# First value product from channel-scaled x, row factor at eviction, and one written order for the keys' end

## The chip, the cores and the metric

The kernel runs on one core of a Trainium2 chip. The metric is the device time of one execution in microseconds (us). Engines are named as in the profile: PE is TensorE's matmul stream and PEld its weight loads, DVE is VectorE, ACT is ScalarE, POOL is GpSimd, SP is SyncE, which only issues transfers. A queue carries its engine's name with a q behind it.

## The reference

One layer of an encoder block, 1024 tokens by 1024 channels, in fp32. The part that matters here is its head:

```python
mod = c_act @ ada_w[l] + ada_b[l]              # c_act = silu(c), one row
sh1, sc1, g1, sh2, sc2, g2 = split(mod, 6)
h = rmsnorm(x, ln1_g[l]) * (1.0 + sc1) + sh1
p = h @ w_in[l]
q, k, v, cb, cc, cx, ga, gb = split(p, ...)
q = rmsnorm(q per head, q_norm_g[l]);  k = rmsnorm(k per head, k_norm_g[l])
```

Behind it come a stick-breaking attention, a short gated convolution, gates, an output projection and a SwiGLU feed-forward part. `rmsnorm` divides each token's row by its root mean square, so `h = r * x * a + sh1` with one factor `r` for a token and one factor `a = ln1_g * (1 + sc1)` for a channel.

## The kernel before

Every product of two fp32 matrices is made from two rounded halves of each side (`hi` and `lo`), as three matmuls: hi by hi, hi by lo, lo by hi. ACT makes a hi, DVE a lo.

The head has these parts. (1) Eight tiles of x, tokens on partitions, are loaded (L173), squared on ACT with a running sum (L242), and give the row factor by a power on POOL (L111). Eight matmuls per half turn the row factors into a row broadcast over all partitions (`bcast`, L249). (2) Per channel tile k, two reductions of 1024 columns on DVE give shift and scale (`mod_sum`, L225, from the transfers `ada`), `norm_x` (L260) multiplies the channel-major x (`xts`) by both factors, `make_hi` and `make_lo` (L265, L269) make the halves of h in the four large tiles `hh` and `hl`. (3) The first value product (512 of 1024 value columns) runs k by k into eight PSUM banks at once: 8 token tiles by 3 matmuls for each k (`real`, L308), the last k token by token, each followed by its eviction and store (`finish_v`, L394). (4) Two key products (two times 512 columns) run token tile by token tile, 24 matmuls each, `finish_k` (L373) behind each: squares on ACT, sums per head on DVE, a power on POOL, `qn` on DVE, four transposes on PE, halves of the key, two stores. (5) `factors` (L341) makes, from x in place, sums and differences of quadrants of h for the gates' seven-product (Strassen-like) scheme and stores four sets as halves (`ts`, three buffers, to `d_t`); h's first half of channels for the later tokens is saved (`d_h`). It is a generator; `more` (L418) takes two or three of its steps behind each key tile. (6) The sets come back as `ft` (two of them before, one after the gates begin) and over the saved half of h. The first gates' two early products (`first_two`, L504, 48 matmuls) need only h.

Instructions are put in order by a planner with its own costs and due times, but for the part from `i0` to L411, which `in_order` (L142) holds in written order on every engine. The planner therefore orders parts (4) to (6). ACT, DVE and POOL take their instructions strictly in the order they are given, and so do the queues.

## Time and profile before

| what | us |
|---|---|
| median of 3 runs (1828.74 to 1829.21) | 1829.14 |
| the profiled execution | 1830.01 |
| its span from first to last instruction | 1828.2 |
| PE busy in the span | 1797.8 |
| DVE busy | 1344.4 |
| ACT busy | 780.1 |

The profiled execution is one run, here 0.9 us above the median. Its own time holds the span and 1.8 us around it. Busy time of PE counts pipelined matmuls whose ends are modelled. The chain of waits follows the work that ended last back to its releasers; it tells which engine a stretch hangs on.

### The profile page before, as it was taken

Reading aid. Unit: us, or ns where it says so; the run is one execution under the profiler, and the core shown is the slowest. Engines: PE = TensorE matmul, PEld = TensorE weight load, DVE = VectorE, ACT = ScalarE, POOL = GpSimd, SP = SyncE. Lnnn points to the kernel's source line nnn. Section 1 sums busy time; section 2 is a strip of 40 time slices with the busy share of each in tenths; the row PEclk is TensorE's granted clock in tenths of the full one; section 3 lists DMA queues with packets and bytes.
Section 4 is the critical chain, followed back from the end, with each engine's and each line's share of the span. In section 5 each row is a group of like instructions: output and inputs, shape, how many; then the busy total and the mean of one; then the engine's idle time right before and its main releaser. Section 6 shows DMA issues by size and latency. Waiting matters only on the chain.

```text
span 1828.2 us, 24681 instructions
## 1 busy us (share of the span) xinstructions
PE 1797.8 (98%) x8765; PEld 1497.7 (82%) x8765; DVE 1344.4 (74%) x1873; ACT 780.1 (43%) x1463; POOL 498.2 (27%) x373
## 2 busy tenths in 40 slices
PE   7999999999999999999999999999999999999999
PEld 5788777888889988888888888878888888878887
DVE  5874686777954888888887584589987788653774
ACT  4342454333344656665655212353443344422320
POOL 0043433833322122211210001335545445200000
PEclk9999999999999999999999999999999999999999
DMA  9688544222738576668544674505443344299776
GB/s 388 212 301 273 192 151 141 93 75 81 259 115 247 145 199 192 187 196 227 160 141 150 217 245 163 174 23 185 184 173 139 138 173 161 93 353 319 279 241 213
DMA packets 148145, 347.23 MB, mean 190 GB/s; under 512 B 15003, under 2 KB 52141, under 8 KB 145846
## 3 DMA queue, kind: packets, MB, share of 16 engines
q1 hardware_dynamic: 112368, 244.79, 41.5%
q10 hardware_dynamic: 30678, 84.61, 12.3%
q0 software_dynamic: 4976, 16.26, 2.4%
q8 instruction: 70, 1.15, 0.3%
q14 instruction: 53, 0.43, 0.1%
HBM read 238.11 MB, written 107.48 MB: 189 GB/s over the span
## 4 chain that ended last, share of the span: by engine, by line
PE 88%; DVE 6%; DMA 2%; issue 2%; ACT 2%; POOL 1%; SPq 0%; DVEq 0%; POOLq 0%; ACTq 0%
PE e L119 7%; PE e L120 7%; PE e L121 7%; PE pj L121 7%; PE pj L119 7%; PE pj L120 7%; PE pj L284 5%; PE e L1506 4%; PE e L1508 4%; PE e L1507 4%; PE tr L817 3%; PE pj L887 3%; PE pj L888 3%; PE pj L889 3%; PE obank L833 2%
## 5 line engine op out<-in xcount | busy, mean ns | idle before, releaser
L802 DVE TENSOR_TENSOR_SCAN pt<-pt,mk 128x128 f32<-128x128 f32 (+7 forms) x128 | 179.6, 1411 | 48.5 <-ACT pt L798 48.1
L124 DVE TENSOR_TENSOR wlo<-raw,whi 128x512 fp32r<-128x512 f32 x148 | 125.5, 857 | 47.4 <-ACT whi L439 35.0
L798 ACT ACTIVATE pt<-z,rq 128x512 f32<-128x512 f32 (+3 forms) x192 | 107.9, 579 | 88.0 <-PE z L797 60.7
L119 PE MATMUL e<-big,whi 128*128 128x512 f32 x352 | 138.1, 392 | 1.1 <-DVE c L124 1.1
L120 PE MATMUL e<-big,whi 128*128 128x512 f32 x352 | 137.7, 391 | 0.0
L121 PE MATMUL e<-big,wlo 128*128 128x512 f32 x352 | 137.5, 391 | 0.0
L124 DVE TENSOR_TENSOR c<-e,c 128x512 f32<-128x512 f32 x154 | 102.9, 681 | 45.2 <-PE e L121 44.0
L124 DVE TENSOR_TENSOR c<-pj,c 128x512 f32<-128x512 f32 x140 | 93.5, 685 | 49.9 <-PE pj L121 49.5
L119 PE MATMUL pj<-big,whi 128*128 128x512 f32 x320 | 125.1, 391 | 0.0
L121 PE MATMUL pj<-big,wlo 128*128 128x512 f32 x320 | 124.9, 390 | 0.0
L120 PE MATMUL pj<-big,whi 128*128 128x512 f32 x320 | 124.6, 389 | 0.0
L1506 PE MATMUL e<-f,whi 128*128 128x512 f32 (+1 forms) x319 | 121.9, 382 | 1.4 <-DMA f<-d_f 1.4
L1507 PE MATMUL e<-f,whi 128*128 128x512 f32 (+1 forms) x319 | 121.9, 382 | 0.0
L1508 PE MATMUL e<-f,wlo 128*128 128x512 f32 (+1 forms) x319 | 121.8, 382 | 0.0
L439 ACT ACTIVATE whi<-raw 128x512 fp32r<-128x512 f32 x116 | 72.7, 629 | 101.6 <-PE pj L120 52.5
L284 PE MATMUL pj<-whi,big 128*128 128x512 f32 x352 | 111.4, 402 | 2.9 <-ACT big L267 2.9
L124 POOL TENSOR_TENSOR ws<-raw 128x512 f32<-128x512 f32 x40 | 61.1, 1527 | 173.0 <-DVE wlo L1108 71.1
L119 PE MATMUL e<-rh,whi 128*128 128x512 f32 x264 | 102.8, 390 | 2.5 <-DVE c L124 2.5
L821 DVE TENSOR_TENSOR atl<-tr,ath 128x512 fp32r<-128x512 f32 (+2 forms) x192 | 98.8, 547 | 8.6 <-ACT ath L820 7.1
L887 PE MATMUL pj<-big,whi 128*128 128x512 f32 x256 | 104.3, 407 | 0.0
L120 PE MATMUL e<-rl,whi 128*128 128x512 f32 x264 | 102.7, 389 | 0.0
L121 PE MATMUL e<-rh,wlo 128*128 128x512 f32 x264 | 102.7, 389 | 0.0
(264 smaller groups left out, 4922.6 us busy)
## 6 DMA issues: line engine op xcount, KB each, us to landing
f<-d_f SPq DMA_DIRECT2D x77, 512.0 KB, 4.3
d_f<-fs ACTq DMA_DIRECT2D x70, 512.0 KB, 2.6
raw<-w_cg SPq DMA_DIRECT2D x40, 512.0 KB, 3.3
ad<-ada ACTq DMA_DIRECT2D x25, 512.0 KB, 4.4
raw<-w_g SPq DMA_DIRECT2D x24, 512.0 KB, 3.8
raw<-w_u SPq DMA_DIRECT2D x24, 512.0 KB, 3.2
ada<-ada SPq DMA_DIRECT2D x8, 1024.0 KB, 11.0
d_t<-ts SPq DMA_DIRECT2D x16, 512.0 KB, 5.1
```

The lines of the kernel that those rows point to most:

```text
L119: nc.tensor.matmul(ps, wh[:, k, :], fh[:, k, :], start=(k == 0), stop=False)
L120: nc.tensor.matmul(ps, wh[:, k, :], fl[:, k, :], start=False, stop=False)
L121: nc.tensor.matmul(ps, wl[:, k, :], fh[:, k, :], start=False, stop=(k == 3))
L124: eng.tensor_tensor(out=out, in0=a, in1=b, op=op)
L284: nc.tensor.matmul(ps, a, b, start=(k == 0 and q == 0), stop=(k == KT - 1 and q == 2))
L798: nc.scalar.activation(pt[:, off + s0:off + s0 + m], z[:, :m], AF.Sigmoid, scale=rq[:, 1, i, h:h + 1])
L802: nc.vector.tensor_tensor_scan(out=pt[:, rev], data0=pt[:, rev], data1=mk[:, rev], initial=1.0, op0=ALU.mult, op1=ALU.max)
L821: nc.vector.tensor_tensor(out=tl[:, :nb, c0:c0 + P], in0=src, in1=th[:, :nb, c0:c0 + P].bitcast(F32), op=ALU.subtract)
L887: nc.tensor.matmul(ps, wh, rh_, start=(k == 0), stop=False)
L1506: nc.tensor.matmul(o, wh, f[:, 0, c], start=(j == 0), stop=False)
L1507: nc.tensor.matmul(o, wh, f[:, 1, c], start=False, stop=False)
L1508: nc.tensor.matmul(o, wl, f[:, 0, c], start=False, stop=(j == NJ - 1))
```

## The change

The first value product is made from `x * a` (the tiles `xa`, hi and lo of x times the channel scale), so it no longer needs the row factor or the shift. The row factor is the scale of the ScalarE copy that evicts each bank (`v_scale`). The shift's share is one row, shift times weights: two lines of 16 matmuls (`bw`), spread over 128 partitions by one fp32 matmul (`bwb`) and added on DVE later (`v_bias`). The conditioning row is loaded as one row and spread by PE; PE runs warming matmuls around that. The transfer of `ada` is cut in scale and shift, the scale's ahead. Squares of x come in between steps of the product. Normalised h is made during the first key product, which now runs k by k like the value product before it. The end of the keys, both the last step of the first and the whole second product, the gates' factors and the first gates' early products stand in one written list, `STEPS`: at each piece c, 6 matmuls are issued and then what the string names. A, M, C, L are the stages of `finish_k` for the first keys, small letters for the second: square and power, normalise, transpose and round, low half, with the store one piece after the low half. f is one step of `factors`, w, r0, r1, r2 and g0, g1 are loads and splits of weights. Two steps of `factors` stand ahead of the list. SP's instructions behind `i1` are left to the planner. Key stores move from SP's queue to ACT's, value stores from ACT's to POOL's.

```diff
-    nc.scalar.activation(one, one, AF.Sigmoid)
+    nc.scalar.activation(one, one, AF.Silu)
...
-    def in_order(i0):
+    def in_order(i0, i1=None):
 
         prev = {}
-        for i in nc.cur_bb.bb.instructions[i0:]:
+        for n, i in enumerate(nc.cur_bb.bb.instructions[i0:]):
+            if i1 is not None and n + i0 >= i1 and i.engine == nc.sync.engine:
+                continue
             if i.engine in prev:
                 tc.add_manual_dep(i, prev[i.engine].name,
...
+    def xa(k, q, ns=slice(0, T)):
+        return xas[k // 2 % 2][:, k % 2, q, ns]
+
...
     cab = sp.tile([P, D], F32, name="cab")
...
-    for i in range(8):
-        nc.sync.dma_start(xq[i], x[i * P:(i + 1) * P, :])
+    row1 = sp.tile([1, P], F32, name="row1")
+    nc.vector.memset(row1, 1.0)
+    nc.scalar.dma_start(cab[0:1], ada_row[0:1, :])
...
+    wq, wraw, ads = [], [], {}
+
+    def load_ada(e, m):
+        ads[e, m] = adp.tile([P, D], F32, tag="ada", bufs=5, name=nm("ada"))
+        nc.sync.dma_start(ads[e, m], ada_1[e, :, m])
...
     def load_x(k):
         nc.sync.dma_start(xt(k), x_t[k])
...
-    def load_ada(e):
-        ad = adp.tile([P, 2, D], F32, tag="ada", bufs=2, name=nm("ada")) if e % 3 < 2 else sp.tile(
-            [P, 2, D], F32, tag="ada", bufs=1, name=nm("ada"))
-        nc.sync.dma_start(ad, ada_1[e])
-        ads.append(ad)
-
...
+    def load_sq(*rows):
+        for i in rows:
+            nc.sync.dma_start(xq[i], x[i * P:(i + 1) * P, :])
...
+    nc.vector.memset(ones2, 1.0)
+    warm = ps_pj()
+
+    def warm_up(n):
+        for i in range(n):
+            nc.tensor.matmul(warm, ident, bws, start=True, stop=True)
+
+    warm_up(3)
+    crow = [ps_pj() for c in range(2)]
+    for c in range(2):
+        nc.tensor.matmul(crow[c], row1, cab[0:1, c * 512:(c + 1) * 512], start=True, stop=True)
+    warm_up(6)
+    nc.vector.tensor_scalar(out=acol1, in0=acol[:, 1], scalar1=1.0, scalar2=None, op0=ALU.add)
+
+    def ada_sum(e, m):
+        nc.vector.tensor_tensor_reduce(out=ads[e, m], in0=ads[e, m], in1=cab, scale=1.0, scalar=0.0, op0=ALU.mult,
+                                       op1=ALU.add, accum_out=msum[:, m, e:e + 1])
+
+    def scale_of(e):
+        ada_sum(e, 1)
+        nc.vector.scalar_tensor_tensor(out=a1[:, e:e + 1], in0=msum[:, 1, e:e + 1], scalar=acol1[:, e:e + 1],
+                                       in1=ln1[:, e:e + 1], op0=ALU.add, op1=ALU.mult)
+
+    def xa_hi(k, ns=slice(0, T)):
+        nc.scalar.activation(xa(k, 0, ns), xt(k)[:, ns], AF.Copy, scale=a1[:, k:k + 1])
+
+    def xa_lo(k, ns=slice(0, T)):
+        nc.vector.scalar_tensor_tensor(out=xa(k, 1, ns), in0=xt(k)[:, ns], scalar=a1[:, k:k + 1],
+                                       in1=xa(k, 0, ns).bitcast(F32), op0=ALU.mult, op1=ALU.subtract)
+
+    def squares(*rows):
+        for i in rows:
+            nc.scalar.activation(xq[i], xq[i], AF.Square, accum_out=ss1[:, i:i + 1])
+
+    def mm_raw(ps, i, k, parts=(0, 1, 2)):
+
+        wh, wl = (v[:, k % 2 * 512:k % 2 * 512 + 512] for v in wq[k // 2])
+        sh, sl = (xa(k, q, slice(i * P, (i + 1) * P)) for q in range(2))
+        for q, (a, b) in enumerate(((sh, wh), (sh, wl), (sl, wh))):
+            if q in parts:
+                nc.tensor.matmul(ps, a, b, start=(k == 0 and q == 0), stop=(k == KT - 1 and q == 2))
+
+    load_ada(0, 1)
+    load_wq(0, 2)
...
+    load_half(0, 0)
     load_x(0)
-    load_wq(0)
-    load_ada(1)
+    load_half(0, 1)
+    load_ada(1, 1)
...
-
-    def mod_sum(e):
-
-        msum = sp.tile([P, 2], F32, tag="msum", bufs=2, name=nm("msum"))
-        for m in range(2):
-            nc.vector.tensor_tensor_reduce(out=ads[e][:, m], in0=ads[e][:, m], in1=cab, scale=1.0, scalar=0.0, op0=ALU.mult,
-                                           op1=ALU.add, accum_out=msum[:, m:m + 1])
-        nc.vector.tensor_tensor(out=mod[:, 0:2, e], in0=msum, in1=acol[:, 0:2, e], op=ALU.add)
-        nc.vector.scalar_tensor_tensor(out=a1[:, e:e + 1], in0=mod[:, 1, e:e + 1], scalar=1.0,
-                                       in1=ln1[:, e:e + 1], op0=ALU.add, op1=ALU.mult)
-
-
-    ss1 = sp.tile([P, 8], F32, name="ss1")
-    rsp = [ps_tr() for n in range(2)]
-    warm = ps_pj()
-    rts = []
-    for i in range(8):
-        nc.tensor.matmul(warm, ident, xq[i][:, :512], start=True, stop=True)
-        nc.scalar.activation(xq[i], xq[i], AF.Square, accum_out=ss1[:, i:i + 1])
-        if i == 5:
-            nc.scalar.activation(rs, cab, AF.Sigmoid)
-            nc.vector.tensor_tensor(out=cab, in0=cab, in1=rs, op=ALU.mult)
-        if i % 4 == 3:
-            rts.append(rstd_of(ss1[:, i - 3:i + 1], 1.0 / D, sp, 4, eng=nc.vector))
+    halves = slice(0, 512), slice(512, T)
+    for c in range(2):
+        nc.scalar.activation(cab[:, halves[c]], crow[c], AF.Silu)
+    split_hi(0)
+    scale_of(0)
+    xa_hi(0, halves[0])
+    xa_hi(0, halves[1])
+    split_hi(1)
+    split_lo(0)
+    for ns in halves:
+        xa_lo(0, ns)
+    scale_of(1)
+    split_lo(1)
+    pss = [ps_pj() for i in range(6)] + [ps_tr() for i in range(2)]
+    rts = [None, None]
+
...
+    def loads(k):
+        if k == 0:
+            load_ada(0, 0)
+            load_ada(3, 1)
+            load_x(3)
+            load_ada(1, 0)
+            load_sq(0)
+            load_ada(4, 1)
+            load_x(4)
+            load_wq(2)
...
+            load_ada(6, 0)
+            load_ada(7, 0)
...
+    rows = {2: (0,), 3: (1, 2), 4: (3,), 5: (4, 5), 6: (6, 7)}
+    for k in range(KT - 1):
+        loads(k)
+        xa_hi(k + 1)
+        if k + 2 < KT:
+            split_hi(k + 2)
+            scale_of(k + 2)
+        squares(*rows.get(k, ()))
+        xa_lo(k + 1)
+        if k + 2 < KT:
+            split_lo(k + 2)
+        if k:
+            ada_sum(k - 1, 0)
+        if k > 4:
+            rts[k - 5] = rstd_of(ss1[:, 4 * k - 20:4 * k - 16], 1.0 / D, sp, 4, eng=nc.vector)
+        for parts in ((0,), (1,), (2,)):
+            for i in range(8):
+                mm_raw(pss[i], i, k, parts)
+
...
+    vs = {i: vpair[n // 2][:, n % 2] for n, i in enumerate((0, 6, 7, 1, 2, 3, 4, 5))}
+    k = KT - 1
+
+    def out_v(i):
+        nc.gpsimd.dma_start(d_v[0][1 + i * P:1 + (i + 1) * P], vs[i])
+
+    def v_scale(i):
+        nc.scalar.activation(vs[i], pss[i], AF.Copy, scale=rts[i // 4][:, i % 4:i % 4 + 1])
+
+    def v_bias(i):
+        tt(nc.vector, vs[i], vs[i], bws, ALU.add)
+        out_v(i)
 
...
     def bcast(n):
+        rsp = ps_tr()
         for i in range(4):
-            nc.tensor.matmul(rsp[n][:, i * P:(i + 1) * P], rts[n][:, i:i + 1].broadcast_to([P, P]), ident,
+            nc.tensor.matmul(rsp[:, i * P:(i + 1) * P], rts[n][:, i:i + 1].broadcast_to([P, P]), ident,
                              start=True, stop=True)
-
-    split_hi(0)
-    hh, hl = [], []
...
-    def norm_x(k, *n):
-        src = xt(k, *n)
-        nc.vector.scalar_tensor_tensor(out=src, in0=src, scalar=a1[:, k:k + 1],
-                                       in1=rsp[n[0]] if n else rs, op0=ALU.mult, op1=ALU.mult)
+        nc.scalar.activation(rs[:, n * 512:(n + 1) * 512], rsp, AF.Copy)
+
+    def norm_x(k):
+        nc.vector.scalar_tensor_tensor(out=xt(k), in0=xt(k), scalar=a1[:, k:k + 1], in1=rs, op0=ALU.mult, op1=ALU.mult)
 
     def make_hi(k, n):
...
 
+    ada_sum(6, 0)
+    ada_sum(7, 0)
+    tt(nc.vector, mod[:, 0], msum[:, 0], acol[:, 0], ALU.add)
+    nc.vector.tensor_copy(out=bhl[:, :, 0], in_=mod[:, 0])
+    tt(nc.vector, bhl[:, :, 1], mod[:, 0], bhl[:, :, 0].bitcast(F32), ALU.subtract)
+
+    def last_raw(*ts):
+        for i in ts:
+            mm_raw(pss[i], i, k)
+            v_scale(i)
+
+    last_raw(0, 6, 7, 1)
     bcast(0)
-    mod_sum(0)
-    load_ada(3)
     bcast(1)
-    norm_x(0, 0)
+    norm_x(0)
     make_hi(0, 0)
-    norm_x(0, 1)
     make_hi(0, 1)
-    split_hi(1)
-    split_lo(0)
-    for n in range(2):
-        make_lo(0, n)
-    for n in range(2):
-        nc.scalar.activation(rs[:, n * 512:(n + 1) * 512], rsp[n], AF.Copy)
-    load_x(4)
-    mod_sum(1)
-    load_ada(4)
-    load_x(5)
+    make_lo(0, 0)
+    last_raw(2, 3)
+    split_hi(8)
+    split_lo(8)
+    bw = ps_pj()
+    for kk in range(KT):
+        for q in range(2):
+            nc.tensor.matmul(bw[:2], bhl[:, kk], wq[kk // 2][q][:, kk % 2 * 512:kk % 2 * 512 + 512],
+                             start=(kk == 0 and q == 0), stop=(kk == KT - 1 and q == 1))
+    last_raw(4)
+    nc.scalar.activation(brow, bw[:2], AF.Copy)
+    last_raw(5)
...
+    w2 = []
     pss = [ps_pj() for i in range(6)] + [ps_tr() for i in range(2)]
 
-    def real(k, i0, i1):
+    def key_step(k):
         for parts in ((0,), (1,), (2,)):
-            for i in range(i0, i1):
-                mm_tok(pss[i], i, wq, k, k + 1, parts)
-
-    for k in range(KT - 1):
-        mc = MC if k else MC0
-        real(k, 0, mc)
-        split_lo(k + 1)
+            for i in range(8):
+                mm_tok(pss[i], i, wq[4:], k, k + 1, parts)
+
+    for k in range(KT - 2):
         for n in range(2):
             make_hi(k + 1, n)
             make_lo(k + 1, n)
-        if k + 2 < KT:
-            split_hi(k + 2)
-            mod_sum(k + 2)
-            norm_x(k + 2)
-        real(k, mc, NPRE)
-        if k % 2 == 0:
-            load_wq(k // 2 + 2)
-        if k + 5 < KT:
-            load_ada(k + 5)
-        if k < 2:
-            load_x(k + 6)
+        norm_x(k + 2)
+        split_hi(k + 10)
+        split_lo(k + 10)
+        for i in ((0, 6), (7, 1), (2, 3), (4, 5))[k] if k < 4 else ():
+            v_bias(i)
...
         nc.vector.tensor_reduce(out=ss, in_=sq.rearrange("p (h d) -> p h d", d=DH), op=ALU.add, axis=AX.X)
-        qn = ap.tile([P, 512], F32, tag="qn", bufs=2, name=nm("qn"))
-        r = rstd_of(ss, 1.0 / DH, ap, 8)
+        r = rstd_of(ss, 1.0 / DH, ap, 8, eng=nc.vector)
+        yield
+        qn = ap.tile([P, 512], F32, tag="qn", bufs=3, name=nm("qn"))
         nc.vector.tensor_tensor(out=qn.rearrange("p (h d) -> p h d", d=DH),
                                 in0=ps.rearrange("p (h d) -> p h d", d=DH),
                                 in1=r.unsqueeze(2).broadcast_to([P, 8, DH]), op=ALU.mult)
...
         nc.scalar.activation(hi, tr, AF.Identity, scale=kgc)
+        yield
         nc.vector.scalar_tensor_tensor(out=lo, in0=tr, scalar=kgc, in1=hi.bitcast(F32), op0=ALU.mult, op1=ALU.subtract)
+        yield
         for e, t in ((0, hi), (1, lo)):
-            nc.sync.dma_start(d_k[e][4 * ch:4 * ch + 4, :, i * P:(i + 1) * P].rearrange("j p t -> p j t"),
+            nc.scalar.dma_start(d_k[e][4 * ch:4 * ch + 4, :, i * P:(i + 1) * P].rearrange("j p t -> p j t"),
                                 t.rearrange("p (j t) -> p j t", j=4).bitcast(F32))
-
-    def finish_v(ps, i):
-        vs = ap.tile([P, 512], F32, tag=("vs", "qn")[i % 2], bufs=3 - i % 2, name=nm("vs"))
-        if i % 2:
-            nc.vector.tensor_copy(out=vs, in_=ps)
-        else:
-            nc.scalar.activation(vs, ps, AF.Copy)
-        nc.scalar.dma_start(d_v[0][1 + i * P:1 + (i + 1) * P], vs)
-
-    tails = []
-    split_w(4)
...
-            next(ml, None)
-
+        yield
+
+    for n in range(2):
+        make_hi(KT - 1, n)
+        make_lo(KT - 1, n)
+    w2.append(load_w(w_kv[2, 2]))
+    next(ml)
+    next(ml)
+    key_step(KT - 2)
+    i1 = len(nc.cur_bb.bb.instructions)
...
-            for tl in tails:
-                next(tl, None)
+    FO = (0, 6, 1, 7, 2, 3, 4, 5)
+    fins, late = {}, []
+    banks = {}
+
+    def act(what):
+        for w in what.split():
+            if w == "f":
+                next(ml, None)
+            elif w == "w":
+                w2.append(load_w(w_kv[2, 3]))
+            elif w == "r0":
+                load_first(0)
+            elif w == "r1":
+                second.append(load_second(0))
+            elif w == "r2":
+                load_first(1)
+            elif w in ("g0", "g1"):
+                split_first(int(w[1]))
+            else:
+                n = int(w[1])
+                key = w[0].isupper(), n
+                if w[0] in "Aa":
+                    ps, i = (pss[FO[n]], FO[n]) if key[0] else (banks[n], n)
+                    fins[key] = finish_k(ps, i, 0 if key[0] else 1)
+                next(fins[key])
+                if w[0] in "Ll":
+                    late.append(key)
...
+
+    second = []
+    STEPS = ("w A0", "f A1 A2", "M0 f", "A3 f", "M1 A4", "f", "C0 L0 M2 A5", "", "M3 A6", "", "C1 M4 L1 A7", "C2 L2 M5",
+             "C3 L3 M6", "C4 L4 M7", "C5 L5 a0", "C6 L6", "C7 L7 m0", "", "c0 l0 a1 f", "f", "m1 f r0", "c1 l1 f", "f r1",
+             "a2 f", "f", "m2 f", "c2 l2 f", "a3 f", "f r2", "m3 f", "f", "c3 l3 f", "f g0", "a4 f", "f", "m4 f f",
+             "c4 l4 a5", "", "m5 a6", "c5 l5 g1", "m6 a7", "c6 l6", "m7", "c7 l7")
+    for c, step in enumerate(STEPS):
+        done, late[:] = list(late), []
+        if c < 4:
+            for i in FO[2 * c:2 * c + 2]:
+                mm_tok(pss[i], i, wq[4:], KT - 1, KT)
+        elif c < 36:
+            i, q = (c - 4) // 4, (c - 4) % 4
+            if q == 0:
+                banks[i] = ps_pj()
+            mm_tok(banks[i], i, w2, 2 * q, 2 * q + 2)
+        else:
+            g, q = (c - 36) // 4, (c - 36) % 4
+            if q % 2 == 0:
+                pre.setdefault(g, []).append(g_bank())
+            half_prod(pre[g][q // 2], early[g][q // 2], *fac[q // 2], q % 2 * 2, q % 2 * 2 + 2)
+        act(step)
+        for key in done:
+            next(fins[key])
+        if c == 35:
+            for _ in ml:
+                pass
+            s2b.close()
+            sx.close()
+            ftx = ExitStack()
+            ftp = ftx.enter_context(tc.tile_pool(name="phft", bufs=1, side="right", reuse_waits="tile"))
+            ft = {q: ftp.tile([P, 2, 4, 512], F32R, name=f"ft{q}") for q in (5, 4)}
+            for q in (5, 4):
+                nc.sync.dma_start(ft[q].bitcast(F32), d_t[q])
+    for key in late:
+        next(fins[key])
+    raw2 = second[0]
+    in_order(i0, i1)
+    zr = ap.tile([1, 512], F32, name="zr")
+    nc.gpsimd.memset(zr, 0.0)
+    for e in range(3):
+        nc.scalar.dma_start(d_v[e][0:1], zr[:, :d_v[e].shape[1]])
 
     def two_raw(g):
```

## Rows read from the trace of the kernel before

**Rows 1.** The page, busy time of the engines over the span.

```profile
PE 1797.8 (98%) x8765; PEld 1497.7 (82%) x8765; DVE 1344.4 (74%) x1873; ACT 780.1 (43%) x1463; POOL 498.2 (27%) x373
```

**Rows 2.** Timeline of PE: start, duration, engine, line, what, count [idle before].

```profile
178.79 0.39 PE L121 MATMUL pj<-big,wlo 128*128 128x512 f32 x1
```

**Rows 3.** Timeline of all engines, first 24 us.

```profile
1.02 0.29 POOL masks.py:199 TENSOR_SCALAR_AFFINE_SELECT dm<-dm 128x128 f32<-128x128 f32 x1
...
4.65 0.15 DVE L96 TENSOR_SCALAR cst<-cst 128x1 f32<-128x1 f32 x1 [3.72 <-DMA cst<-cols]
...
10.51 0.34 PEld L241 LDWEIGHTS pj<-xq,dm 128*128 128x128 f32 x1 [0.52 <-DMA xq<-x]
...
11.36 0.34 PEld L241 LDWEIGHTS pj<-xq,dm 128*128 128x128 f32 x1 [0.52 <-issue]
...
12.13 0.19 PEld L241 LDWEIGHTS pj<-xq,dm 128*128 128x128 f32 x1 [0.43 <-DMA xq<-x]
12.56 0.19 PEld L241 LDWEIGHTS pj<-xq,dm 128*128 128x128 f32 x1 [0.24 <-issue]
...
16.57 1.05 PE L251 MATMUL tr<-dm,rs_r 128*128 128x128 f32 x8
...
23.61 1.65 PE L284 MATMUL pj<-whi,big 128*128 128x512 f32 x3 [1.05 <-ACT big L267]
```

**Rows 4.** Stages: busy us of PE, PEld, DVE, ACT, POOL, granted clock, DMA.

```profile
23.61:68.29 44.68, 42.80 (x171) 33.31 (x171) 42.55 (x73) 14.80 (x25) 0.52 (x1) 0.94 0.67 267
...
101.46:166.69 65.23, 65.23 (x313) 53.88 (x312) 36.90 (x55) 24.43 (x40) 22.75 (x24) 1.00 0.94 313
```

**Rows 5.** The chain of waits: start, duration, what.

```profile
46.80 1.29 DVE xts L262
...
53.00 1.29 DVE xts L262
...
73.58 27.88 PE pj L284 x123
...
137.29 0.44 PE tr L386 x4
...
143.19 0.44 PE tr L386 x4
```

**Rows 6.** Groups of instructions, 0 to 130 us: busy us, mean ns, idle before.

```profile
L229 DVE CUSTOM_DVE_ANT_0 ada<-ada,cab 128x1024 f32<-128x1024 f32 x16 | 18.9, 1220 | 0.0
L111 POOL TENSOR_TENSOR rs_r<-rs_m,nhalf 128x8 f32<-128x8 f32 x9 | 15.1, 1679 | 0.8
...
L242 ACT ACTIVATE xq<-xq 128x1024 f32<-128x1024 f32 x8 | 8.4, 1048 | 6.6 <-PE pj L241 6.6
```

**Rows 7.** One-microsecond slice of PE: busy time, granted clock, DMA.

```profile
23.00:24.00 1.00, 0.39 (x1) 0.50 1.11 455
```

**Rows 8.** Timeline of DVE in the first key product.

```profile
97.77 0.68 DVE L380 TENSOR_TENSOR qn<-pj,rs_r 128x512 f32<-128x512 f32 x1
98.37 0.74 DVE L348 SCALAR_TENSOR_TENSOR xts<-xts,mod 128x512 f32<-128x512 f32 x1
99.03 0.68 DVE L377 TENSOR_REDUCE qss<-qsq 128x8 f32<-128x512 f32 x1
```

**Rows 9.** The stored factor halves (tile ts): waits for the store, time to landing.

```profile
  DMA d_t<-ts: 3.5, 6
...
DMA to landing us min/median/max: 3.1/5.1/7.3
```

**Rows 10.** Timeline of SP's queue, the factors' transfers.

```profile
135.49 1.18 SPq L354 DMA_DIRECT2D d_t<-ts  x1
138.41 0.33 SPq L488 DMA_DIRECT2D ft<-d_t  x1
```

**Rows 11.** The loaded factors (tile ft), time to landing.

```profile
DMA to landing us min/median/max: 9.0/9.0/9.0
```

**Rows 12.** Stages of 5 us, columns as in rows 4.

```profile
145.00:150.00 5.00, 5.00 (x26) 4.14 (x25) 1.11 (x3) 0.84 (x2) 1.55 (x1) 1.00 1.05 400
```

More of the change, by code (lines that the diff above doesn't have):

```diff
@@ new lines, in block_kernel @@
+    load_wq(7)
+    hh = [big(), None]
+    hl = [big(), None]
+    hh[1], hl[1] = big(), big()
+    vpair = [adp.tile([P, 2, 512], F32, tag="ada", bufs=5, name=nm("vs")) for n in range(4)]
+    vs = {i: vpair[n // 2][:, n % 2] for n, i in enumerate((0, 6, 7, 1, 2, 3, 4, 5))}
[7 more added lines that the diff above has]
+        out_v(i)
@@ L496, in block_kernel @@
     pre = {}
-    def first_two(g):
-        if g not in early:
-            split_first(g)
-        return [g_prod(early[g][c], c) for c in range(2)]
-    for g in range(NG):
-        pre[g] = first_two(g)
-        if g == 0:
-            for tl in tails:
-                next(tl, None)
+    FO = (0, 6, 1, 7, 2, 3, 4, 5)
[24 more added lines that the diff above has]
+                    late.append(key)
```

121 lines of the change are left out of this document (53 added, 68 removed).

## Prediction

> **What bounds the kernel now.** I read the page first, then the stretch of the edit in four views: the busy time of stages, the chain of waits, the timelines of the engines, and the DMA queue. TensorE is busy nearly all of the span [rows 1], so only gaps in its stream can be given back. The edit touches the stretch from the start to the last matmul of the early gate products, which begins at 178.79 [rows 2], so that the next could begin at 179.0. In it TensorE's useful stream begins at 23.61 [rows 3]. From there to 68.29 VectorE is busy 42.55 of 44.68 us and the granted clock is below full [rows 4]; the chain of waits runs through VectorE, and two successive normalisations lie 6.20 us apart (46.80 and 53.00) [rows 5]. After that the matmuls run back to back: 123 of them in 27.88 us, 0.2267 us each, so a step of 24 takes 5.44. A key tile with its four transposes has a period of 5.90 (137.29 to 143.19) [rows 5], so the transposes cost 0.46.
>
> The useful work from 23.61 is 3 x 192 + 48 = 624 matmuls (141.5 us) and 16 sets of transposes (7.4): 148.9. It took 155.4. So the stretch loses 23.6 us ahead of the first product and 6.5 inside, nearly all in the first value product.
>
> **The start.** The squares of x and their row factor no longer stand ahead of the first product. What stands there now on TensorE is 3 warming matmuls, 2 that spread the conditioning row over the partitions, and 6 more, 11 in fp32 and so 22 passes. The identity is ready at 1.31, so they begin near 1.5. A pass of this size took 0.85 us (10.51 to 11.36) and later 0.43 (12.13 to 12.56) [rows 3]; from 7.79 on about five were slow. With five slow and 17 fast: 4.3 + 7.3 = 11.6, first product at 13.1. All fast gives 11.0, all slow 20.2. The other chain is shorter: the row is a transfer issued beside the constants, which were there at 4.65 [rows 3]; its two matmuls end near 8, then two halves of SiLU and the reduction of one ada tile (1.22) [rows 6], the scale and the first rounded half of x add about 3 us, 11. The six warming matmuls, queued ahead of the product in TensorE's order, then set the start. I take 13.1.
>
> The clock: before, the first products ran at a granted 0.50, the lower level of 1.2 GHz [rows 7], after TensorE had stood idle behind the row factor. The new queue leaves no such idle. Should it fall all the same, a dozen products cost about 2.6 us more.
>
> **The value product.** VectorE's list per step becomes two ada reductions (2.5), the scale (0.2), the low half of scaled x (1.2) and the weights' low half (0.6), 4.5 us, under the 5.44 of TensorE; before it was 6.2. Starts of neighbouring operations lie 0.60 and 0.66 apart, less than their busy times [rows 8], so I use those. ScalarE has at most one rounded half of a whole row (1.05), one of weights (0.6) and two squares of 1.05 with their read-out [rows 6], 4.1 us. The loads are 20 MB as before, reordered; at 0.4 MB per us the last x tile lands near 41 and is needed near 50. The 6.5 inside are therefore gone.
>
> **Between the products.** The eviction by row factor is the ScalarE copy of before, now with a scale. New on TensorE: the shift times the weights, 16 matmuls of 512 columns (3.6); spreading two lines over 128 rows (0.9); the row-factor broadcast, which moves from the start into the stream, 1.05 for four [rows 3], 2.1 for both; and about 0.5 of waiting where the spread row and the last eviction must come through ScalarE first. Nothing lies under these: 7.1. The eight bias additions (0.6 each) and the v stores, which move to GpSimd's queue, lie under key steps: 4.4 of VectorE against 5.44.
>
> Without further waits the last early gate product ends at 13.1 + 148.9 + 7.1 = 169.1 instead of 179.0, a gain of 9.9.
>
> **The keys' end.** Here the written order matters. Normalising x for the keys now fills the first seven key steps, so all but two of the factor operations, at an f in the list of 44 pieces, move behind them: four in pieces 1 to 5 and 18 from piece 18 to 35. Pieces 18 to 35 are 18 x 1.36 + 4 x 0.46 = 26.3 us of TensorE. VectorE has there four key reductions with their mean (0.72), four normalisations (0.60), four low halves (0.66), 24 factor instructions (nine at 0.66, 15 at 0.60) and a split (1.2): 24.0 us. It fits only if it does not wait. It must not lag by more than two pieces either, since a key's transposes come two pieces after its normalisation, and the power for that takes 1.68 on GpSimd [rows 6]. Two waits are built in. Each low half waits for that piece's transposes. And the four stores of a factor group use three buffers within two pieces, so the fourth copy waits for the first store: these landed in 3.1 to 7.3 us, median 5.1 [rows 9]. Behind that ScalarE copy stand the next square and the rounded keys; behind these, VectorE's reductions; and TensorE waits for their result. Worked through piece by piece with 3.1 per store, this adds about 1 us up to piece 17 and up to 8 to the end, 9 in all. On the other side, before, six of 16 copies waited 3.5 us in all [rows 9], 0.6 a time, which for four groups is 2.4. Nothing excludes zero. That row is the nearest one, the same copies and stores; I take 3.5 and keep 0 to 9.
>
> **The factors' loads.** The last factor store comes at piece 35 instead of at 135.49, and the loads of the first two factor sets, before from 138.41 on, follow it [rows 10]. Before, they had some 40 us until the first product that needed them; now eight pieces, 10.9 us, and four sets of transposes, 1.8. One such load of 2 MB landed in 9.0 [rows 11]. That is just in time for the first set. Three more sets follow; each has a product of 2.7 us in between, one with none of the four. I take 1 us; the ends are 0 and 9, worked out below.
>
> **Sum.** Gain 9.9 - 3.5 - 1 = 5.4. The profiled execution took 1830.0 for a span of 1828.2, so 1824.6 of the same kind. The median of the runs shown, 1829.14, is 0.9 lower: 1823.7, say 1824. Behind the stretch nothing changes but one more load of an activation table on ScalarE (about 1.3 us, under matmuls); a shift of the start passes through to the end because the gates behind it keep TensorE full. A difference under 0.2% (3.7 us) I call no change.
>
> **Rival one: the written order eats it.** The waits of the keys' end come to their upper end of 9 with the loads in time: 9.9 - 9 = 0.9, 1828. For it: VectorE and ScalarE take every piece in order, and 24 of 26 us leaves no room. Against it: before, VectorE was busy only 36.90 of 65.23 us from 101.46 on [rows 4], so the work itself has room over the whole stretch.
>
> **Rival two, the slow side: the factors arrive late.** From the last factor operation to the product with the last set, TensorE has 10.9 + 1.8 + 10.9 = 23.6 us. In that time four sets (8 MB), the saving of the half of h that one set overwrites (2 MB), the last factor store (0.5) and some 2 MB of key stores must move. At the 400 GB/s of a busy slice [rows 12] 12.5 MB take 31 us, and the store must land before the first load starts: 8 to 9 us late. With 5 for the order, 9.9 - 5 - 9 = -4, 1833; with both at their ends, 1837. It decides once more than about 9 MB must pass in that gap. For it: before, the same transfers were spread over 138 to 187 and slices there stood at 400 GB/s. Against it: the key stores may be late themselves, the save can go early, and the product without new factors stands third.
> The Trainium skill, "DMA: Bandwidth & Descriptors", section on queues, rings and completion order, says that each transfer engine takes turns between the queues it has work for. The key stores and the save now stand on ScalarE's queue, the factor loads on SyncE's. By that rule the move to another queue buys no bandwidth, and the late rival stands at its price, 1833; were the queues independent, 8 MB would take 20 us and the forecast would stand. No row here separates the queues in that stretch.
>
> **Rival three: the start is not earlier.** If all 22 warming passes ran slow, the product would begin at 20.2: 2.8 gained before any wait, 1831 with 4.5 of them. Against it: the same passes sped up by 12.13 before.
>
> **Chances.** Forecast (gain above 3.7, the waits at their lower half): 0.47. Rival one and small mixtures, within 3.7: 0.22. Rival two above 3.7 of loss: 0.26. Rival three: 0.05, of which about half counts as same. So faster 0.47, same 0.25, slower 0.28. The range goes from the case without waits and with a somewhat earlier start, 1818, to rival two, 1834; below lies under 0.1, above about 0.1. The likeliest case alone: 1818 to 1826.
>
> **What would show it.** First product from scaled x at 11 to 14; value steps 5.4 apart with no gap; the two broadcasts and 16 narrow products between 56 and 64; TensorE's idle in the keys' end, put down to the normalised keys or key banks, 2 to 5 us in all; the first gate product with loaded factors with a wait for DMA under 2. If instead TensorE waits for loaded factors for 5 us or more, rival two holds; if the waits on normalised keys sum to 8, rival one. A start later than 15 or a granted clock of 0.5 after it would make the first step wrong.

## The result and the profile after

The changed kernel takes 1854.41 us, the median of four runs (1852.85 to 1855.43), against 1829.18 for the kernel before beside it: a ratio of 1.0137, 95% interval 1.0120 to 1.0155. It is slower by 25.2 us, outside the range of 1818 to 1834. The profiled execution took 1852.85 for a span of 1851.1.

The first steps went as worked out. TensorE's timeline of the changed kernel has the first product from scaled x at 13.50, where [rows 3] had 23.61, and the narrow products of the shift, the spreading of the row and the first key step follow with 0.57 us of idle time (in brackets: idle time before, and what ended it):

```profile
1.77 5.04 PE L228 MATMUL pj<-bws,dm 128*128 128x512 f32 x6 [1.77 <-DVE bws L222]
6.74 1.98 PE L233 MATMUL pj<-cab,row 1*128 1x512 f32 x4
8.65 5.42 PE L228 MATMUL pj<-bws,dm 128*128 128x512 f32 x12
13.50 1.73 PE L263 MATMUL pj<-whi,xa 128*128 128x512 f32 x5
...
63.74 1.12 PE L427 MATMUL pj<-brow,ones 2*128 2x512 f32 x2 [0.57 <-ACT brow L421]
64.79 1.45 PE L392 MATMUL pj<-whi,big 128*128 128x512 f32 x5
...
116.45 0.47 PE L392 MATMUL pj<-whi,big 128*128 128x512 f32 x1 [1.77 <-DVE qn L500]
...
140.68 0.63 PE L506 MATMUL tr<-dm,qn 128*128 128x128 f32 x4 [1.23 <-DVE qn L500]
...
151.03 0.63 PE L506 MATMUL tr<-dm,qn 128*128 128x128 f32 x4 [2.90 <-DVE qn L500]
...
168.21 0.63 PE L506 MATMUL tr<-dm,qn 128*128 128x128 f32 x4 [2.44 <-DVE qn L500]
...
176.21 0.63 PE L506 MATMUL tr<-dm,qn 128*128 128x128 f32 x4 [3.25 <-DVE qn L500]
178.14 0.80 PE L119 MATMUL pj<-big,whi 128*128 128x512 f32 x1 [1.29 <-ACT whi L542]
...
187.78 0.63 PE L506 MATMUL tr<-dm,qn 128*128 128x128 f32 x4 [0.82 <-DVE qn L500]
...
202.63 0.80 PE L119 MATMUL pj<-ft,whi 128*128 128x512 f32 x1 [14.22 <-ACT whi L542]
```

From 116 on the reader sees what took the gain back: seven waits of TensorE, six on the key finishes and one on a split, 13.7 us together, and then 14.22 us in front of the first product with loaded factors (tile `ft`, the start of the gates). That product began at 179.44 in the trace of before. From it to the end of the span the two kernels are alike: 1851.1 - 202.63 = 1648.5, and 1828.2 - 179.44 = 1648.8. The whole loss lies ahead of 202.63.

The stages, with the columns of [rows 4]:

```profile
64.00:104.00 40.00, 40.00 (x175) 32.47 (x175) 32.36 (x43) 17.77 (x28) 5.05 (x9) 1.00 0.46 158
...
104.00:172.00 68.00, 59.65 (x286) 48.29 (x285) 47.82 (x83) 26.17 (x45) 23.36 (x13) 1.00 0.66 211
172.00:203.00 31.00, 11.41 (x42) 8.20 (x41) 10.68 (x24) 8.35 (x16) 9.92 (x7) 0.69 1.03 383
```

Up to 172 us the transfer engines have a third of their time free, where before they were busy 0.94 [rows 4]; then they are full for 31 us, and TensorE waits. The granted clock falls in that stretch: the matmuls behind the waits that end at 178.14 and 202.63 run at 0.43 us each for about a dozen, instead of 0.23.

Who issued those transfers shows on SyncE's queue, first, and on ScalarE's queue with its operations, second:

```profile
110.43 61.12 SPq L473 DMA_DIRECT2D d_t<-ts  x16
172.39 0.57 SPq L632 DMA_DIRECT2D ft<-d_t  x1
175.04 3.29 SPq L767 DMA_DIRECT2D big<-d_t  x2
180.50 0.32 SPq L632 DMA_DIRECT2D ft<-d_t  x1
197.45 0.32 SPq L765 DMA_DIRECT2D ft<-d_t  x1
```

```profile
169.66 0.34 ACTq L487 DMA_DIRECT2D d_h<-big  x1
170.04 1.20 ACTq L488 DMA_DIRECT2D d_h<-big  x1
...
178.38 7.14 ACTq L514 DMA_DIRECT2D d_k<-khl  x1
...
189.52 7.57 ACTq L514 DMA_DIRECT2D d_k<-khl  x2
197.14 0.69 ACT L509 ACTIVATE khl<-tr,cst 128x512 fp32r<-128x512 f32 x1 [10.88 <-DMA d_k<-khl]
...
200.91 2.18 ACT L542 ACTIVATE whi<-ws 128x512 fp32r<-128x512 f32 x4
```

The factor loads start at 172.39 (138.41 in [rows 10]) and meet the save of h's half and the last key stores. Two issues on ScalarE (one store, then a pair) take over 7 us each, the last rounded key waits 10.88 us for an earlier key store, and the gates' split, which TensorE waits for, stands behind it. The chain of waits says the same in two pieces:

```profile
172.79 23.86 DMA d_k<-khl
...
202.63 0.80 PE pj L119
```

So the 14.22 us are not a wait for the loads. TensorE's last transposes begin at 187.78 and end near 188.4; the last rounded key begins at 197.14, 8.7 us later; and from there ScalarE has 5.5 us of work (two key stores to issue, copies, splits of the gates' weights) until the product at 202.63. Before, ScalarE's work behind the last rounded key took 3.9 us and cost 0.27, because 16 early gate matmuls stood behind the last transposes and ran meanwhile:

```profile
174.90 0.60 PE L386 MATMUL tr<-dm,qn 128*128 128x128 f32 x4
...
175.53 0.69 ACT L389 ACTIVATE khl<-tr,cst 128x512 fp32r<-128x512 f32 x1 [1.59 <-PE tr L386]
...
177.71 2.20 ACT L439 ACTIVATE whi<-ws 128x512 fp32r<-128x512 f32 x4
...
179.44 0.50 PE L119 MATMUL pj<-ft,whi 128*128 128x512 f32 x1 [0.27 <-ACT whi L439]
```

In the written list the last transposes stand behind the last early gate matmul, so nothing runs over that work.

In the trace of before, the save of h's half went out at 84.35 and the first of the sixteen factor stores at 89.66. The changed kernel issues them at 169.66 and 110.43.

### The profile page after: what moved, and what is told of

It reads as the page before. It is cut to its first block, busy times and chain, and to the rows that moved or that the text cites. A ratio compares the mean times of both kernels' runs of the same rounds, so it can differ in the third digit from the quotient of the medians.

```text
span 1851.1 us, 24753 instructions
## 1 busy us (share of the span) xinstructions
PE 1806.9 (98%) x8789; PEld 1502.0 (81%) x8789; DVE 1360.0 (73%) x1903; ACT 795.5 (43%) x1484; POOL 500.7 (27%) x365
## 3 DMA queue, kind: packets, MB, share of 16 engines
q10 hardware_dynamic: 46280, 90.38, 13.4%
## 4 chain that ended last, share of the span: by engine, by line
PE 89%; DVE 4%; DMA 3%; issue 2%; ACT 1%; POOL 1%; ACTq 0%; SPq 0%; DVEq 0%; POOLq 0%
PE e L119 7%; PE e L120 7%; PE e L121 7%; PE pj L119 7%; PE pj L121 7%; PE pj L120 7%; PE e L1639 4%; PE e L1640 4%; PE e L1641 4%; PE tr L950 3%; PE pj L1020 3%; PE pj L1021 3%; PE pj L1022 3%; PE pj L392 2%; PE obank L966 2%; PE pj L263 2%
## 5 line engine op out<-in xcount | busy, mean ns | idle before, releaser
L124 DVE TENSOR_TENSOR wlo<-raw,whi 128x512 fp32r<-128x512 f32 x164 | 136.4, 841 | 49.6 <-ACT whi L542 34.0
L119 PE MATMUL pj<-ft,whi 128*128 128x512 f32 x240 | 96.1, 400 | 14.2 <-ACT whi L542 14.2
```

Of the source, the lines that this page charges most:

```text
L119: nc.tensor.matmul(ps, wh[:, k, :], fh[:, k, :], start=(k == 0), stop=False)
L124: eng.tensor_tensor(out=out, in0=a, in1=b, op=op)
```

## The experiments

All ran beside the kernel before, in four rounds: e1, e2, e5 and e6; e7 to e9; e10 to e13; e14 to e16. The kernel before had medians of 1828.8 to 1830.2 in them, so a difference between runs of different rounds is good to about 1.5 us. Behind each time stand its ratio to the kernel before in its own round and the 95% interval. The start of the first product with loaded factors ("gates at") is from each one's profile.

**The place of the save (e2) and the queue of the key stores (e1).** My first theory was that the save of h's half, ahead of the key stores in ScalarE's queue, holds them up; its rival, that the factor loads take the engines' bytes whatever the queues.

```
+            nc.scalar.dma_start(d_h[k - 4], (hh, hl)[k - 4][1][:, :4].bitcast(F32))   # e2: in key steps 4, 5
...                                                                                  # e2: not behind piece 35
-            nc.scalar.dma_start(d_k[e]...
+            nc.sync.dma_start(d_k[e]...                                              # e1
```

> The save of half of h (2 MB) is issued on ScalarE's queue in the fifth and sixth key step instead of at piece 35, so it no longer stands ahead of the last five keys' stores in that queue. First theory (stores behind the save in one queue): the wait of 14.2 us ahead of the first product with loaded factors falls under 3, the slower clock behind it goes too, and the time falls by 13 to 19 us, to 1836 to 1841. Second theory (the 8 MB of factor loads take the engines, whatever stands in ScalarE's queue): the last key stores still land 10 us or more after issue, the wait stays above 8, and the time falls by less than 6. Third theory (the order of the list alone costs the loss): no change but noise.

> Only the queue of the 32 key stores goes back from ScalarE's to SyncE's. First theory: ScalarE is no longer held while issuing (7.1 and 7.6 us now) and the stores are not behind the save, so the 14.2 us wait falls under 5 and the time to 1836 to 1842. Second theory: the stores now stand behind the factor loads in SyncE's queue, land 10 us late or more as before, the buffers of the rounded keys come free as late, and the time stays within 5 of 1854.

e2: 1853.54 (ratio 1.0137, 1.0120 to 1.0153), gates at 202.12 behind 16.98 us of wait. e1: 1853.81 (1.0133, 1.0118 to 1.0148); TensorE now waits for the loads themselves:

```profile
198.84 0.77 PE L119 MATMUL pj<-ft,whi 128*128 128x512 f32 x1 [13.28 <-DMA ft<-d_t]
```

The first theory falls, and the second's expectations hold in both. In e2 the key stores land late, in e1 the loads, and the time is the same within 1 us of the changed kernel.

**The planner's order for the keys' end (e5) and a shorter start (e6).**

```
-            if i1 is not None and n + i0 >= i1 and i.engine == nc.sync.engine:
+            if i1 is not None and n + i0 >= i1:        # e5: the list binds no engine from i1 on
-    warm_up(6)
+    warm_up(2)                                          # e6
```

> The instructions behind the last but one key step are no longer held in written order on any engine; the planner orders them as it did before. If the written order costs what the waits of TensorE on normalised keys and banks show (13.8 us) and brings about the late save and its 14.2, both go, and the time is 1824 to 1834, near the sum of the start's gain. If the pieces themselves are tight whatever their order (three buffers for the factor halves, loads after the last factor), it stays above 1844.

> Four of the six warming matmuls behind the spread row are left out; they compute nothing that is used. If they set the start, the first product comes at about 11.7 instead of 13.5 and, as nothing up to the keys' end has slack to take it up, the time falls by 1 to 2 us. If the clock falls in the gap of about 1 us that they leave, or the first product waits for its operands as long, the start stays at 13 or later and the time does not fall.

e5: 1840.68 (1.0066, 1.0046 to 1.0087), gates at 187.71, between its two expectations. So about 14 of the 25.2 us come with the written list, and about 11 with the rest of the change. The list's share holds more than the waits inside it: in e5 the factor loads also start earlier, at 141.64. TensorE's two longest waits in e5:

```profile
114.97 0.77 PE L392 MATMUL pj<-whi,big 128*128 128x512 f32 x1 [6.30 <-DVE rs_m L110]
...
187.71 0.79 PE L119 MATMUL pj<-ft,whi 128*128 128x512 f32 x1 [6.61 <-ACT whi L542]
```

e6: 1853.85 (1.0132, 1.0116 to 1.0147). Its first product starts at 12.34, behind a wait of 1.05 for the rounded scaled x, and its gates at 201.42; the time is within 1 us of the changed kernel.

**The ring of three store buffers (e7), and the factors early (e8, e8g).** The factors are made in pairs of operation and split, one to a piece of the list:

```
+                nc.scalar.activation(ts[:, 0], o, AF.Copy)
+                if open_:
+                    rest(*open_)          # subtraction and store of the factor before
+                open_ = ts, o, q, j
+                yield
```

In e7 they stand in pieces 1 to 34. In e8 they stand in pieces 1 to 24, the loads follow piece 26 instead of 35 and h's half is saved as in e2. In e8g GpSimd makes the subtraction.

> Each factor is followed at once by its own split, copy and store, one factor to a piece, spread over pieces 1 to 34 instead of four copies in a row behind four subtractions; the drain, the save of h's half and the loads of the factors stay behind piece 35. Theory one (the written order costs TensorE time of its own, through the ring of three store tiles: ScalarE waited 10.9 us there): the copies stop waiting for stores, TensorE's 9.1 us of idle time between 116 and 176 us falls to about 4, the factor loads start about 5 us earlier and the whole comes out 4 to 7 us under the changed kernel, 1847 to 1850. Rival (VectorE's own work in the last key step sets the pace, not the ring): ScalarE's waits go but TensorE's idle time stays within 2 us, 1852 to 1855.

> The same pairs, but the sixteen factors are done by piece 24 and the loads of the factors are issued behind piece 26 instead of 35; the save of h's half goes into key steps 4 and 5. Theory two (the wait before the gates is the factor loads' start plus some 11 MB at about 0.4 MB a us): the loads start about 15 to 20 us earlier, the 14.2 us wait and the half-clock passes behind it go, 1826 to 1836. Rival (the wait is not the loads' start but the key stores' small packets, which come when they come): the wait stays above 8 us, 1843 to 1852. Second rival: VectorE has no room for factors and finishes together, and TensorE's idle time in pieces 0 to 24 grows by what the end wins: 1840 to 1850 with the idle time early.

> As the kernel before it, with the subtraction of the split (sixteen, 688 ns each on VectorE) on GpSimd. If VectorE's work sets the pace in pieces 0 to 24: 11 us of it move away and the time falls by 3 to 8 us under that kernel. If not (or if GpSimd's passes of about 1.4 us take as much through later stores): within 2 us of it.

e7: 1855.49 (1.0135, 1.0120 to 1.0150). ScalarE's waits for factor stores fell from 10.9 to 5.8 us and TensorE's seven waits only from 13.7 to 11.3. The loads were issued at 171.38, the gates began at 203.17: what the order gave back was waited for at the end (18.55 us). Shorter waits at the ring alone gain nothing.

e8: 1845.61 (1.0080, 1.0064 to 1.0096), loads from 160.42, gates at 193.87 behind 5.66 us instead of 14.22. None of its three expectations fits whole: the loads' start carries through, yet they started 12 us earlier and the time fell by 9 to 10; ScalarE's issue of a pair of key stores still took 4.92 us at 172.90. e8g: 1851.84 (1.0112, 1.0097 to 1.0127), 6 us worse than e8: either VectorE was not short of those 11 us, or GpSimd took more back. TensorE's waits on the key finishes are 13.2 us in its trace and 9.4 in e8's. GpSimd also makes the power that each key finish needs; that this is why was not tried.

**Fewer bytes (e9, e12).** These leave out part of the computation: e9 the save and reload of h's half and the fourth factor set, e12 all four factor sets, with standing halves of h in the products instead.

```
-        nc.sync.dma_start(fac[3][e].bitcast(F32), d_t[3][:, e])      # e9, e12
-        nc.scalar.dma_start(d_h[0], hh[1][:, :4].bitcast(F32))       # e9, with its pair and the reload
-    nc.sync.dma_start(ft[6].bitcast(F32), d_t[6])                    # e12
-                nc.sync.dma_start(ft[q].bitcast(F32), d_t[q])        # e12
```

> The changed kernel without the save of h's half, its reload later, and the load of the fourth factor set (2 MB each), so that one of the gates' seven products takes h's half in its stead. Theory two (bytes at the engines' rate set the wait): 4 MB fewer in the stretch, 9 to 11 us less wait in front of the gates, 1841 to 1845. Rival (the key stores' place in their queue, or the order on the engines, sets it): the wait stays within 3 us, 1849 to 1854.

> The changed kernel without any of the loads of the four factor sets (8 MB); the gates' products take the half of h that stands ready in their stead. Nothing else is changed: the factors are still made and stored, h's half is still saved, the key stores keep their queue. Theory two (these loads, issued from 172 us on, are what the gates and the key stores wait for): the key stores land in under 5 us again, ScalarE's issue is no longer blocked, the 14.2 us wait and the half-clock passes go, the gates start at about 186 to 189 us instead of 202.6 and the whole takes 1836 to 1841, which leaves the written order's own waits. Rival (the end of the keys' chain on ScalarE and VectorE sets the gates' start): the wait stays above 8 us, 1847 to 1854.

e9: 1847.38 (1.0088, 1.0071 to 1.0105), gates at 196.51: 7 to 9 us for 4 MB, and between the two expectations: the wait in front of the gates itself fell only from 14.22 to 11.46, as the rival had it. e12: 1842.48 (1.0074, 1.0059 to 1.0089), gates at 192.48, time and gates both later than theory two had them. Without the loads the issue of a key store takes 1.17 us at most, and the stores of the rounded keys (tile khl, shortest, median and longest landing, from 170 us) take

```profile
DMA to landing us min/median/max: 2.4/5.1/7.9
```

where the changed kernel has, from 170 us on and then over all its key stores,

```profile
DMA to landing us min/median/max: 9.4/12.6/17.4
DMA to landing us min/median/max: 2.4/2.8/17.4
```

So the loads cost about 12 us of the 25. (This share and the list's 14 overlap, since the list also sets when the loads start.) Without any loads 5.38 us of wait in front of the gates are left, more than a third of the 14.22: there the last rounded key begins at 187.13, as soon as its transposes are done, and the gates 5.35 later, behind ScalarE's last work.

**Both at once (e10, e13, e11).** e10 is e5 with the key stores on SyncE's queue and the early save; e13 is e10 with the list kept on TensorE, VectorE and ScalarE up to piece 12 and the rest left to the planner; e11 is e8 with the key stores on SyncE's queue.

```
-            if i1 is not None and n + i0 >= i1 and i.engine == nc.sync.engine:
+            if i1 is not None and n + i0 >= (i1 if i.engine == nc.sync.engine else i2):   # e13, i2: piece 12
```

> The start of the changed kernel with the planner's order behind key step 6, as in the kernel that came to 1840.7, and with the key stores on SyncE's queue and the save of h's half in key steps 4 and 5. If ScalarE's blocked issue is what is left of its end wait (6.6 us at 187.7): that wait falls to 2 to 4 us, 1836 to 1839. If the engines' byte rate is: within 2 us of 1840.7.

> As that one, but the written order is kept on TensorE, VectorE and ScalarE up to piece 12 of the keys' end and the planner orders what follows. If the 6.3 us of idle TensorE at 115 in the planner's version come from factors put ahead of the key finishes, they fall to the list's 1 to 2 us, and the time to 1832 to 1837. Rival: the factors come later by it, so the loads start later and the wait before the gates takes it back, 1838 to 1846.

> The written order with the factors done by piece 24 and loads behind piece 26 (1845.6 before), and with the key stores on SyncE's queue. If ScalarE's issues (4.9 us blocked at 173, 9 us in all) hold up the last finishes, the wait before the gates and TensorE's waits on the last transposes fall by 4 to 6 us, 1839 to 1842; if the bytes set the end, within 2 us of 1845.6.

e10: 1838.42 (1.0052, 1.0037 to 1.0067), gates at 184.22; TensorE's wait at 115 grew to 7.58 us while the last one shrank to 3.94. e11: 1839.31 (1.0057, 1.0042 to 1.0072), 6.3 below e8, or 4.9 when each is taken against the kernel before in its own round: the move of the key stores, worth nothing in e1, pays once the loads are earlier. e13: 1835.15 (1.0030, 1.0018 to 1.0043), gates at 183.28 behind 7.71, its early waits 2.18 and 1.61. All three times lie in the range of their first expectation, though e10's 2.3 us below e5 are within e5's spread (1838.2 to 1844.3). The stages of e13 show the transfer engines nearly full from 115 on and full from 130:

```profile
115.00:130.00 15.00, 13.39 (x66) 10.81 (x65) 10.52 (x20) 8.62 (x16) 4.36 (x4) 1.00 0.91 314
130.00:145.00 15.00, 15.00 (x77) 12.44 (x76) 13.40 (x26) 7.43 (x13) 8.93 (x5) 1.00 1.03 338
145.00:160.00 15.00, 15.00 (x78) 12.47 (x77) 6.66 (x12) 2.67 (x4) 4.18 (x3) 1.00 1.02 317
160.00:170.00 10.00, 10.00 (x50) 8.30 (x49) 4.47 (x8) 3.04 (x5) 1.64 (x1) 1.00 1.07 365
170.00:180.00 10.00, 5.57 (x29) 4.43 (x27) 2.65 (x5) 2.00 (x4) 6.63 (x5) 0.94 1.04 347
```

**What bounds that version (e14, e15, e16).** e14 is e13 without the loads of the third and fourth factor sets (4 MB; two products take standing halves of h). e15 is e13 with the shorter start of e6. e16 adds the early pairs and loads of e8 to it.

> The mixed order (1835.15) without the loads of the third and fourth factor sets (4 MB), whose products take the halves of h that stand ready. If the bytes set the end of that version: the engines move 0.33 to 0.4 MB a us there, so the 7.7 us wait before the gates falls by all of it or nearly, the half-clock passes with it, 1825 to 1829. If the order on ScalarE and VectorE does: within 2 us of 1835.

> The mixed order with two warming matmuls instead of six ahead of the first product. If TensorE's start still passes through to the end: 1.5 to 2.5 us less, 1833 to 1834. If the bytes of the later window set the end: within 1 us of 1835, since the factors' stores hang on VectorE and not on TensorE's start.

> That one, with the factors in pairs of factor and split and all but the last ones in the written pieces up to 24, the loads behind piece 26, so that stores begin at about 97 instead of about 107 us. If the start of the factors' traffic is what counts: 3 to 8 us less, 1826 to 1831, level with before. If VectorE has no room for it, within 2 us of 1835.

e14: 1832.61 (1.0015, 1.0005 to 1.0024), gates at 180.06: 2.5 us of time for 4 MB, where the byte rate alone would give 10 to 12. But of these 4 MB e13 issues 2 only at 181.33, just ahead of its gates. The wait of e14 in front of the gates fell from 7.71 to 3.94, and what is left is not bytes:

```profile
176.15 0.69 ACT L508 ACTIVATE khl<-tr,cst 128x512 fp32r<-128x512 f32 x1 [2.45 <-PE tr L505]
...
178.33 2.19 ACT L541 ACTIVATE whi<-ws 128x512 fp32r<-128x512 f32 x4
...
180.06 0.79 PE L119 MATMUL pj<-ft,whi 128*128 128x512 f32 x1 [3.94 <-ACT whi L541]
```

The last rounded key waits for nothing but its own transposes, and then ScalarE's last work takes 3.9 us, as it did before, with no early gate matmul left to run over it. The wait in e10 and in e11 is 3.94 as well, and ends the same way.

e15: 1835.48 (1.0029, 1.0018 to 1.0040), level with e13. e16: 1834.20 (1.0024, 1.0015 to 1.0033), 1 us below e13, within the runs' spread; TensorE comes to the end of its key products sooner and waits longer there:

```profile
180.61 0.79 PE L119 MATMUL pj<-ft,whi 128*128 128x512 f32 x1 [9.15 <-ACT whi L540]
```

In e15 and e16 a TensorE that is earlier gains nothing that the times show. In all three the last rounded keys wait for stores of earlier keys, 13 to 17 us from 160 on (14.1 in e14). No version beats the kernel before; the best that compute everything, e13, e15 and e16, stand 0.24% to 0.30% above it, and e14, which leaves out loads, 0.15%.

## Why the prediction was wrong

**Right: the start, the value product, the part between.** First product at 13.50, predicted 13.1; value steps without a gap at full granted clock; the first key step at 64.79, where the steps gave 13.1 + 43.5 + 7.1 = 63.7. The key steps then run back to back. By the forecast's own sum TensorE was ahead by about 9 us at the start of the list (its 9.9 less the 1.1 lost so far).

**Wrong: "I take 3.5 and keep 0 to 9" for the keys' end.** It measured 13.7 of idle time, above the upper end, and about 2.4 more where a dozen passes ran at half the clock behind the wait at 178.14. The landing time was not at fault: the stores landed in 3.1 to 4.2 us, under the 3.1 to 7.3 of [rows 9]. The nearest row, six waits of 0.6 [rows 9], came from an order that the planner had chosen around the landings; in the written order four copies waited 10.9 us. My piece by piece working said 9, and I set it aside for that row. It was the better guide. Nor was the ring all of it: e7 halved its waits and TensorE got 2.4 us. Against the planner's order (e5) the list costs about 14 us, of which a part falls in front of the gates.

**Wrong: "I take 1 us" for the factors' loads.** The wait in that place measured 14.2. The working counted from an end of the list that came in time and, for the forecast, one load of 9.0 us by itself [rows 11]. With the save, three of the four sets (6 MB; the fourth went out at 197.45) and the last key stores at once, the loads landed in 13.4 (median) and the key stores in up to 17.4. By that median, the two first sets, issued at 172.39 and 180.50, were there near 194; what came last was ScalarE. The term had no place for two things: 8.7 us in which the last rounded key waited for key stores and for ScalarE, which was still issuing them, and 5.5 us of ScalarE's work behind it with TensorE idle. The kernel before had hidden 3.9 us of that work under matmuls, and the forecast put it at nothing. e12, without the loads, keeps 5.38 of it.

The terms explain the miss: 0.4 and 0.7 before the key steps, 10.2 + 2.4 at the keys' end and 13.2 in front of the gates are 26.9 of the 28.2 us between 1824.6 and the profiled execution, 1852.85. About a dozen half-clock passes behind 202.63 cost 2.4 more there, but they are no part of the loss, since from 202.63 on the span is no longer than before.

**Rivals one and two both came true, and both were priced too low.** Rival one's sign, waits on normalised keys of 8 us, came at 12.4. Rival two named the bytes (12.5 MB in 23.6 us) and came to 8 or 9 us late, 1833, and 1837 with both ends. Its sign, TensorE waiting for loaded factors, shows only in e1 (13.28). What it missed is how late transfers act: not by the loads alone, but by key stores that stand between them, whose buffers the last rounded keys need, and by an issuing ScalarE that stands still. The rule it cited from the Trainium skill, "DMA: Bandwidth & Descriptors", section "Queues, rings and completion order", is that the engines take turns between the queues. The forecast drew from it that another queue buys no bandwidth, which fits e1, 1853.81 against the 1854.41 of the changed kernel. In e11 the other queue did pay, 5 to 6 us; there ScalarE no longer issues key stores and so cannot stand still at them, but that this is the reason is argued and not shown.

**Behind it: the change moves the traffic, not only TensorE.** The stretch moves about the same bytes in both kernels, 25.8 MB from 90 to 179 us before and 26.2 MB from 104 to 203 after. Before, x was normalised early, so that h's half and the first factors left from 84 on, under key products. Now x for the keys is normalised in the key steps, and the factors start when these end: the engines are busy 0.46 from 64 to 104 and 0.66 from 104 to 172. I worked TensorE's path out to a tenth of a microsecond and the traffic only from piece 35 on. e8 (loads earlier, -9 to -10), e9 and e12 (bytes taken out, -7 to -9 and -12) and e13 (order and traffic, -19) show it.

**Still open** is how the 5 or 6 us of the best versions above before divide. The traces name three parts: the 3.9 us of ScalarE's last work that no early gate matmul covers any more, the waits of the rounded keys for key stores (e13 waits 7.71 in front of the gates, e14 with 4 MB less 3.94), and the half-clock passes behind that wait. None was taken away by itself: the last transposes were not put ahead of early gate matmuls again, and more buffers for the rounded keys, or fewer, larger stores, were not tried. Nor do the runs say why TensorE waits longer inside the list than in the planner's order (13.7 us against 8.0 in e5), beyond the ring's share.

## What to carry to other kernels

When a change makes one engine earlier, list the transfers of the stretch with the earliest moment each can start, and compare the bytes left from there with the time left; a gain on TensorE ahead of a full transfer window is only a longer wait. A written order of three engines should be costed by its own worked chain, not by waits measured under a planner's order, and to the end of the chain: ask what the other engines still have to do behind TensorE's last instruction, and what TensorE runs meanwhile. And do not hold big loads for the end of such a list: each small store still to come then pays for them.

## What was not expected of the hardware

- Issuing can block: a key store took ScalarE 0.37 us to issue in the quiet part and 7.14 and 7.57 us beside the 2 MB loads (the second figure is of a pair), and ScalarE's next rounded keys began only as these issues ended (185.57 and 197.14). Without the loads (e12) the longest was 1.17. What the issue waits for, no run shows.
- The key stores, 256 KB each in packets of about 500 B (16,896 for the 8.39 MB of their queue in the trace of e9), suffer more beside 2 MB loads than these do: from 170 us on their median landing was 12.6 and the longest 17.4 us, against 2.8 in the median over all of them and 5.1 in e12 without the loads, while that of the loads went from 9.0 [rows 11] to 13.4.
- A few us of idle TensorE cost more than themselves: behind the waits of 3.25 and 1.29 us, and again behind the 14.22, the granted clock stood at 0.50, the lower level of 1.2 GHz (178.2 to 183.4 and 202.7 to 207.4), and a dozen matmuls took 0.43 instead of 0.23 us. Behind the single waits of 2.90 and 2.44 us, earlier in the list, they took 0.23.
